# The second feed-forward layer's up products by seven products instead of eight

## The chip, the cores and the metric

The kernel runs on one core of a Trainium2 chip. The metric is the device time of one execution in microseconds; lower is better. A core has five engines with a queue of instructions each: PE multiplies matrices, DVE (VectorE), ACT (ScalarE) and POOL (GpSimd) work on elements, SP starts DMA transfers. An engine takes its queue in order; engines wait for each other by semaphores. SBUF is the working memory of 128 partitions; PSUM, with eight banks here, takes what PE writes.

## The reference

Two layers, each a mixer (pooling in the first, sparse attention in the second) and a gated feed-forward network (FFN) with a causal convolution of width 3. The tokens are 512 of a prompt (`hp`) and 8 x 8 new ones of running sequences (`hs`), 576 in all. The change concerns the FFN of the second layer.

```python
ALPHA = (2.0 * DEPTH) ** 0.25            # DEPTH = 2, D_MODEL = 1024, D_FF = 2816, CONV_W = 3
...
def conv_ffn(x, prefix, w_up, conv_w, conv_b, w_down):
    T = x.shape[1]
    up = x @ w_up                        # 1024 -> 2 * 2816: gate columns, then value columns
    up_pad = jnp.concatenate([prefix, up], 1)
    c = conv_b
    for k in range(CONV_W):
        c = c + conv_w[k] * up_pad[:, k:k + T]
    g, u = jnp.split(c, 2, -1)
    y = (jax.nn.silu(g) * u) @ w_down
    return y, up_pad[:, -(CONV_W - 1):]
...
        hp = layer_norm(ALPHA * hp + mp, ln_g[i, 0], ln_b[i, 0])
        hs = layer_norm(ALPHA * hs + ms, ln_g[i, 0], ln_b[i, 0])
        fp, nfp = conv_ffn(hp, zeros, ffn_w_up[i], ffn_conv_w[i], ffn_conv_b[i], ffn_w_down[i])
        fs, nfs = conv_ffn(hs, state_ffn[i], ffn_w_up[i], ffn_conv_w[i], ffn_conv_b[i], ffn_w_down[i])
        hp = layer_norm(ALPHA * hp + fp, ln_g[i, 1], ln_b[i, 1])
        hs = layer_norm(ALPHA * hs + fs, ln_g[i, 1], ln_b[i, 1])
```

## The kernel before

All products are in single precision made of parts: a matrix is split into a high part (a copy in the reduced type fp32r, by ACT) and a low part (the matrix less its high part, by DVE), and one product is three matmuls: high by high, high by low, low by high. The method `Units.split` with `pieces` (lines 247 and 248) splits weights, `mm3` (line 168) issues the matmuls. A matmul has a 128 x 128 block of weights standing and 288 tokens moving, which is half of the 576.

`x` lies transposed, features on partitions: `xz` is the residual (8 blocks of 128 features by 576 tokens), `xh` and `xl` its parts. In the first layer and in the second the function `ffn` does the same. The 2816 hidden features are 22 chunks of 128. `up` takes chunks by twos: it loads 256 gate columns and 256 value columns of the up weights (1024 KB each, one DMA each, into one of two raw buffers), splits them in pieces of 128 x 2048, and makes for each chunk, half of the tokens and side (gate or value) one bank of PSUM out of 8 blocks x 3 = 24 matmuls, so 96 matmuls for a chunk. `conv` copies the banks by ACT into the padded row buffer `u` (lines 405 to 407; four buffers), saves the last rows (POOL, line 408), and does the convolution: one ACT instruction (line 412) and two of DVE (413, 414) for each side. Then come SiLU (437, ACT), the product of the sides (438, DVE), and the split of the result into `hh` and `hl` (447 ACT, 448 DVE; eight buffers each).

`down` multiplies groups of four chunks (the last: six) with the down weights: for 8 blocks of output features and 2 halves of tokens 12 matmuls (the last: 18), and adds each bank to `xz` by DVE (line 494). The order is up of chunks 0 to 3, then up of the next four and down of the four before them, and so on; at the end up of 20 and 21 and the down of 16 to 21. During the first two chunks the layer norm of the second half of the tokens is still finished (`opening`), and during the last down the final norm of the first half is done (`closing`, from `final_norm`): it scales and shifts the rows `xn` with POOL on 352 of the columns and DVE on 672 at the same time (line 1606).

The program is written as a sequence of tiles and instructions; a planner then sets each engine's order from its own costs and the order of writing, and puts in the waits. `Slots` gives tiles of a tag in turn from a fixed number of buffers; a tile's next use waits until the last reader of the one before is done. PSUM tiles come from one pool of eight banks (`mmt`).

## Time and profile before

| | us |
|---|---|
| median of three runs | 1707.0 (1706.89 to 1708.22) |
| profiled execution, own time | 1708.67 |
| its span, first to last instruction | 1706.9 |
| PE busy | 1638.8 (96%) |
| DVE busy | 1046.9 (61%) |
| ACT busy | 816.3 (48%) |
| POOL busy | 426.5 (25%) |

The profile is one execution with start and length of each instruction. Busy time counts what the engine's units do; waiting for a semaphore is idle time, but what holds up an instruction after its start lengthens it. Matmuls overlap each other, so their spacing, not their length, says what one costs. The second FFN takes the stretch from about 1254 to 1686 us.

### The profile page before, as it was taken

To read this page: it belongs to the slowest core of one execution; us is meant where nothing else is said; L and a number is where in the kernel's file an instruction comes from. 1 tells how busy PE (TensorE), PEld (TensorE's weight loads), DVE (VectorE), ACT (ScalarE), POOL (GpSimd) and SP (SyncE) were. 2 spreads that over 40 slices of the span, in tenths; PEclk is the share of its full clock that TensorE was granted. 3 is DMA by queue.
4 is the path that set the end of the run, shared out by engine and by line. 5 is a ranking of instruction groups with operands and counts; after the bars stand their busy time and mean duration, and the time that the engine had idled before them with its cause. 6 is when DMAs were issued, how large, how long until landed. Compare 5 with 4: busy or idle time off the path is not lost. (4 is left out here: it accounts for less than half of the span.)

```text
span 1706.9 us, 31668 instructions
## 1 busy us (share of the span) xinstructions
PE 1638.8 (96%) x12711; PEld 1555.0 (91%) x12711; DVE 1046.9 (61%) x2162; ACT 816.3 (48%) x1499; POOL 426.5 (25%) x606
## 2 busy tenths in 40 slices
PE   7999999999999989999999988999999999999995
PEld 7999999999999989999956667887999999999995
DVE  7766464545574347889755558898466545454547
ACT  5654334343353314655654447888256534344331
POOL 2222121111020013333312216766023202111104
PEclk9999999999999999999999999999999999999998
DMA  5233132223247736544659941002512222222211
GB/s 190 83 100 100 55 111 83 75 75 99 63 167 214 229 119 244 187 167 164 208 182 350 342 124 26 1 12 69 153 50 75 78 96 75 84 90 81 93 60 56
DMA packets 130850, 206.02 MB, mean 121 GB/s; under 512 B 25775, under 2 KB 106761, under 8 KB 120336
## 3 DMA queue, kind: packets, MB, share of 16 engines
q1 hardware_dynamic: 120800, 134.49, 25.0%
q0 software_dynamic: 9216, 67.11, 11.1%
q8 instruction: 100, 1.64, 0.4%
q10 hardware_dynamic: 688, 2.40, 0.4%
q14 instruction: 46, 0.38, 0.1%
HBM read 179.63 MB, written 24.84 MB: 120 GB/s over the span
## 5 line engine op out<-in xcount | busy, mean ns | idle before, releaser
L168 PE MATMUL u<-xl,wha 128*128 128x288 f32 x704 | 208.0, 296 | 0.3 <-POOL xl L342 0.2
L168 PE MATMUL u<-xl,whb 128*128 128x288 f32 x704 | 208.0, 296 | 0.2
L168 PE MATMUL u<-xh,whb 128*128 128x288 f32 x704 | 207.3, 295 | 0.0
L168 PE MATMUL u<-xh,wha 128*128 128x288 f32 x704 | 207.3, 295 | 0.0
L168 PE MATMUL u<-xh,wlb 128*128 128x288 f32 x704 | 207.3, 295 | 0.0
L168 PE MATMUL u<-xh,wla 128*128 128x288 f32 x704 | 207.2, 295 | 0.0
L408 POOL COPY fcol<-u 128x18 f32<-128x18 f32 x88 | 69.4, 798 | 467.1 <-ACT u L407 467.0
L413 DVE SCALAR_TENSOR_TENSOR c<-u,convp,c 128x592 f32<-128x592 f32 x88 | 72.2, 831 | 122.2 <-ACT c L412 122.2
L248 DVE TENSOR_TENSOR wla<-rawa,wha 128x2048 fp32r<-128x2048 f32 (+1 forms) x52 | 99.5, 1918 | 68.7 <-ACT wha L247 68.0
L248 DVE TENSOR_TENSOR wlb<-rawb,whb 128x2048 fp32r<-128x2048 f32 x37 | 84.8, 2292 | 83.4 <-ACT whb L247 83.4
L168 PEld LDWEIGHTS u<-xl,wha 128*128 128x128 f32 x704 | 132.0, 188 | 2.0 <-DVE xl L342 1.1
L168 PEld LDWEIGHTS u<-xl,whb 128*128 128x128 f32 x704 | 132.0, 188 | 1.9 <-DVE xl L342 1.1
L168 PEld LDWEIGHTS u<-xh,whb 128*128 128x128 f32 x704 | 132.0, 188 | 0.1
L168 PEld LDWEIGHTS u<-xh,wha 128*128 128x128 f32 x704 | 132.0, 188 | 0.1
L168 PEld LDWEIGHTS u<-xh,wlb 128*128 128x128 f32 x704 | 132.0, 188 | 0.0
L168 PEld LDWEIGHTS u<-xh,wla 128*128 128x128 f32 x704 | 132.0, 188 | 0.0
L247 ACT ACTIVATE wha<-rawa 128x2048 fp32r<-128x2048 f32 (+1 forms) x52 | 83.0, 1615 | 91.1 <-PE d L168 58.9
L247 ACT ACTIVATE whb<-rawb 128x2048 fp32r<-128x2048 f32 x37 | 70.9, 1915 | 113.5 <-DMA rawb<-in_ffn_w_up 41.0
L494 DVE SCALAR_TENSOR_TENSOR xz<-xz,d 128x288 f32<-128x288 f32 x160 | 70.1, 450 | 85.5 <-PE d L168 84.8
L901 PE MATMUL pr<-xhi,W1h 128*128 128x256 f32 x512 | 105.6, 288 | 10.2 <-ACT xhi L874 10.2
L874 ACT ACTIVATE xhi<-xf 128x1024 fp32r<-128x1024 f32 (+1 forms) x68 | 70.1, 1031 | 83.1 <-PE pr L901 46.0
L168 PE MATMUL d<-hh,wha 128*128 128x288 f32 x352 | 104.4, 298 | 0.1
(779 smaller groups left out, 4900.6 us busy)
## 6 DMA issues: line engine op xcount, KB each, us to landing
rawa<-in_ffn_w_up SPq DMA_DIRECT2D x22, 1024.0 KB
rawb<-in_ffn_w_up SPq DMA_DIRECT2D x22, 1024.0 KB
rawa<-in_ffn_w_down SPq DMA_DIRECT2D x11, 1024.0 KB
rawb<-in_ffn_w_down SPq DMA_DIRECT2D x11, 1024.0 KB
rawa<-in_nsa_w_in SPq DMA_DIRECT2D x9, 1024.0 KB
sr<-in_state_win_kv SPq DMA_DIRECT2D x8, 1024.0 KB
out_win_kv_s<-sr SPq DMA_DIRECT2D x8, 1008.0 KB
rawb<-in_nsa_w_o SPq DMA_DIRECT2D x16, 256.0 KB
```

Source lines behind the costliest of these rows:

```text
L168: pe.matmul(out, a, b, start=first and j == 0, stop=last and j == n - 1)
L247: act.activation(h[:, a:b], r[:, a:b], AF.Copy)
L248: dve.tensor_tensor(lo[:, a:b], r[:, a:b], f32(h[:, a:b]), OP.subtract)
L408: pool.tensor_copy(col[:, :, m].rearrange("p (j i) -> p j i", i=2), u[:, TP:TP + 90].rearrange("p (j i) -> p j i", i=10)[:, :, 0:2])
L413: dve.scalar_tensor_tensor(c, u[:, 1:1 + CW], cv[:, 44 + m:45 + m], c, OP.mult, OP.add)
L494: dve.scalar_tensor_tensor(z, z, ALPHA if first else 1.0, p_[:, :HALF], OP.mult, OP.add)
L874: act.activation(xhi.rearrange(flat), xf.rearrange(flat), AF.Copy)
L901: pe.matmul(banks[b, kv][ri][:, :, gh * nn:(gh + 1) * nn], W1[wi][:, kv, ri * 8 + th * 4 + c], xx[:, c // 2, c % 2].rearrange("p g n -> p ...
```

## The change

The second layer's FFN becomes `ffn_seven`; the first keeps `ffn`. For chunks 2 to 21 the product of a 2 x 2 block matrix of weights (gate and value rows by two halves of the 1024 input features) with a 2 x 2 block matrix of tokens (two halves of the features by two halves of the tokens) is made with seven block products in place of eight, by sums and differences of blocks (the scheme of Strassen in Winograd's form). Each block product is 4 blocks x 3 = 12 matmuls of the same form as before. Chunks 0 and 1 (`up_plain`) are made with eight, and after them `token_sums` makes three combinations of the token blocks, once, in the raw buffers `u`.

For each chunk the weights come as four pieces of 128 x 512 (256 KB, one DMA each), POOL makes four combinations of them, and seven pieces are split by ACT and DVE. The pieces go through `Ring`: eight buffers for raw pieces and combinations, twelve pairs for the parts. Of the seven banks ACT copies three to SBUF; DVE makes three sums with a bank and one with a copy, and POOL and DVE put the four quarters of the result into `u`. The down weights come through the same ring in pieces of 128 x 512 (256 KB; the last down of 128 x 384, loaded anew for each half of the tokens). `hh` and `hl` get six buffers in place of eight. The order is up of 0 and 1, token sums, up of 2 to 5, then four times a down of four and an up of four, and the last down of six.

To make room, the constants behind `band` move to a tile that lives from the middle of the projection of the second layer on, with their DMA there, and the rows of the norms (`xn`) and the final norm's factors `gb` come from pools that are opened and closed around the chunks 2 to 21.

```diff
+HB = 6
+YB = 1
...
-    cst = cp.tile([128, CONSTS.shape[1] - (COFF["band"][1] - COFF["band"][0])], F32, name="cst")
     K0, K1 = COFF["band"]
+    cst = cp.tile([128, K0], F32, name="cst")
...
+    class Ring:
+        ORDER = "r" * 8 + "hl" * 12
+        def __init__(self, ctx, key):
+            self.slots, self.turn, self.n, self.key = {x: [] for x in "rhl"}, {x: 0 for x in "rhl"}, 0, key
+            for j, tag in enumerate(self.ORDER):
+                self.slots[tag].append(mkpool(ctx, f"ring{key}{tag}{j}"))
+        def slot(self, tag):
+            own = self.slots[tag]
+            j = self.turn[tag]
+            self.turn[tag] = (j + 1) % len(own)
+            self.n += 1
+            return own[j].tile([128, 512], F32 if tag == "r" else F32R, tag=tag, name=f"w{tag}{self.key}{self.n}")
+        def fetch(self, src):
+            _, k, n = src.shape
+            raw = self.slot("r")[:, :k * n]
+            sp.dma_start(raw.rearrange("p (k n) -> p k n", k=k), src)
+            return raw
+        def combine(self, a, b, op, out=None):
+            out = self.slot("r") if out is None else out
+            pool.tensor_tensor(out, a, b, op)
+            return out
+        def split(self, raw):
+            n = raw.shape[1]
+            h, lo = (self.slot(x)[:, :n] for x in "hl")
+            act.activation(h, raw, AF.Copy)
+            dve.tensor_tensor(lo, raw, f32(h), OP.subtract)
+            return tuple(t.rearrange("p (k n) -> p k n", n=128) for t in (h, lo))
...
+    def ffn_seven(l, R, ctx, opening, closing, no_norm, last_norm):
+        fp = Slots(ctx, f"ffn{l}")
+        cv = convp[l]
+        xz, xh, xl = X["z"], X["h"], X["l"]
...
+        half = [slice(0, HALF), slice(HALF, T)]
+        ks = [slice(0, 4), slice(4, 8)]
+        wv = I["ffn_w_up"][l].rearrange("(k p) n -> p k n", p=128)
+        def quarter(k, n):
+            return xh[:, ks[k], half[n]], xl[:, ks[k], half[n]]
+        def block(bank, w, x, first=True, last=True):
+            terms = [(w[wi][:, k], x[xi][:, k]) for k in range(4) for wi, xi in ((0, 0), (0, 1), (1, 0))]
+            mm3(bank[:, :HALF], terms, first, last)
+        def pieces(m):
+            return [R.fetch(wv[:, ks[k], c:c + 128]) for c in (m * 128, FF + m * 128) for k in range(2)]
...
+        def rows(m, q):
+            u = fp.tile([128, UW + 8], F32, tag="u", name=f"u{l}{q * NF + m}", bufs=4)
+            us = u[:, 2 + TP:UW].rearrange("p (b t) -> p b t", t=2 + TS)
+            pool.memset(u[:, 0:2], 0.0)
+            pool.tensor_copy(us[:, :, 0:2], sTv[:, :, q * NF + m].rearrange("p (b k) -> p b k", k=2))
+            return u, us[:, :, 2:]
...
+            hh = fp.tile([128, T], F32R, tag="hh", name=f"hh{l}{m}", bufs=HB)
+            hl = fp.tile([128, T], F32R, tag="hl", name=f"hl{l}{m}", bufs=HB)
...
+        def up_plain(ms):
+            w = {m: [R.split(p_) for p_ in pieces(m)] for m in ms}
+            banks = {}
+            for i, (n, m, q) in enumerate((n, m, q) for n in range(2) for m in ms for q in range(2)):
+                b = banks[m, n, q] = mmt(f"u{l}{m}{n}{q}")
+                for k in range(2):
+                    block(b, w[m][2 * q + k], quarter(k, n), k == 0, k == 1)
+                opening(i)
+            for m in ms:
+                us = []
+                for q in range(2):
+                    u, s = rows(m, q)
+                    act.activation(u[:, 2:2 + HALF], banks[m, 0, q][:, :HALF], AF.Copy)
+                    act.activation(u[:, 2 + HALF:2 + TP], banks[m, 1, q][:, :TP - HALF], AF.Copy)
+                    act.activation(s, samples(banks[m, 1, q]), AF.Copy)
+                    us.append(u)
+                gated(m, *us)
...
+        def token_sums(ctx):
+            tp_ = mkpool(ctx, f"tsum{l}", side="right")
+            z = [[xz[:, ks[k], half[n]] for n in range(2)] for k in range(2)]
+            t = {n: tuple(tp_.tile([128, 4, HALF], F32R, name=f"t{n}{x}{l}") for x in "hl") for n in (1, 2, 3)}
+            t[4] = quarter(0, 1)
+            for k in range(4):
+                raws = [fp.tile([128, UW + 8], F32, tag="u", name=f"ts{l}{k}{i}", bufs=4) for i in range(2)]
+                r = {n: raws[n % 2][:, i * HALF:(i + 1) * HALF] for i, ns in enumerate(((3, 2), (1, 4))) for n in ns}
+                for n, a, b in ((3, z[1][1][:, k], z[0][1][:, k]), (1, z[0][1][:, k], z[0][0][:, k]),
+                                (2, z[1][1][:, k], r[1]), (4, z[1][0][:, k], r[2])):
+                    (pool if n == 3 else dve).tensor_tensor(r[n], a, b, OP.subtract)
+                for n in (3, 2, 1, 4):
+                    act.activation(t[n][0][:, k], r[n], AF.Copy)
+                    dve.tensor_tensor(t[n][1][:, k], r[n], f32(t[n][0])[:, k], OP.subtract)
+            xt.update(t)
+        def up(m):
+            a11, a12, a21, a22 = pieces(m)
+            s1 = R.combine(a21, a22, OP.add)
+            s3 = R.combine(a11, a21, OP.subtract, a21)
+            s2 = R.combine(s1, a11, OP.subtract)
+            s4 = R.combine(a12, s2, OP.subtract)
+            w = {n: R.split(x) for n, x in (("a11", a11), ("s3", s3), ("s2", s2), ("a12", a12), ("a22", a22), ("s1", s1), ("s4", s4))}
+            (ug, sg), (uu, su) = rows(m, 0), rows(m, 1)
+            def product(n, wn, x):
+                bank = mmt(f"u{l}{m}p{n}")
+                block(bank, w[wn], x)
+                return bank
+            def copied(n, wn, x):
+                bank = product(n, wn, x)
+                out = fp.tile([128, HALF], F32, tag=f"y{n}", name=f"y{n}{l}{m}", bufs=YB)
+                act.activation(out, bank[:, :HALF], AF.Copy)
+                return out
+            def second(eng, u, us, a, b):
+                eng.tensor_tensor(u[:, 2 + HALF:2 + TP], a[:, :TP - HALF], b[:, :TP - HALF], OP.add)
+                eng.tensor_tensor(us, samples(a), samples(b), OP.add)
+            p1 = copied(1, "a11", quarter(0, 0))
+            p7 = copied(7, "s3", xt[3])
+            b6 = product(6, "s2", xt[2])
+            y = fp.tile([128, HALF], F32, tag="y", name=f"y{l}{m}", bufs=YB)
+            dve.tensor_tensor(y, p1, b6[:, :HALF], OP.add)
+            b2 = product(2, "a12", quarter(1, 0))
+            dve.tensor_tensor(ug[:, 2:2 + HALF], p1, b2[:, :HALF], OP.add)
+            pool.tensor_tensor(p7, y, p7, OP.add)
+            b4 = product(4, "a22", xt[4])
+            dve.tensor_tensor(uu[:, 2:2 + HALF], p7, b4[:, :HALF], OP.add)
+            p5 = copied(5, "s1", xt[1])
+            second(pool, uu, su, p7, p5)
+            pool.tensor_tensor(p5, y, p5, OP.add)
+            b3 = product(3, "s4", quarter(1, 1))
+            second(dve, ug, sg, p5, b3)
+            gated(m, ug, uu)
...
+        def down(chunks, first, last):
+            subs = [chunks] if len(chunks) == 4 else [chunks[:3], chunks[3:]]
+            wts = {}
+            for hf, m in ([(hf, m) for hf in range(2) for m in range(KD)] if last else [(hf, m) for m in range(KD) for hf in range(2)]):
+                if last or hf == 0:
+                    wts[m] = [R.split(R.fetch(I["ffn_w_down"][l][sub[0] * 128:(sub[-1] + 1) * 128, m * 128:(m + 1) * 128]
+                                              .rearrange("(k p) n -> p k n", p=128))) for sub in subs]
+                p_ = mmt(f"d{l}{m}{hf}{chunks[0]}")
+                mm3(p_[:, :HALF], [(wt[wi][:, k], hp[c][xi][:, half[hf]]) for sub, wt in zip(subs, wts[m])
+                                   for k, c in enumerate(sub) for wi, xi in ((0, 0), (0, 1), (1, 0))])
+                z = xz[:, m, half[hf]]
+                dve.scalar_tensor_tensor(z, z, ALPHA if first else 1.0, p_[:, :HALF], OP.mult, OP.add)
...
+        up_plain([0, 1])
+        no_norm()
+        with ExitStack() as c1:
+            token_sums(c1)
+            ups([2, 3])
+            ups([4, 5])
+            for g in range(4):
+                down(list(range(4 * g, 4 * g + 4)), g == 0, False)
+                ups(list(range(4 * g + 6, 4 * g + 10)))
+        last_norm()
         down(list(range(16, 22)), False, True)
...
+        N["cst"] = p_.tile([128, CONSTS.shape[1] - K1], F32, name="cstr")
+        sp.dma_start(N["cst"], I["consts"][:, K1:])
...
-    def final_norm(sp_, U):
-        gb = U.raw()[:, :2048].rearrange("p (s c) -> p s c", s=2)[:LT]
-        sp.dma_start(gb[:, 0], I["ln_g"][1, 1].unsqueeze(0).broadcast_to([LT, D]))
-        sp.dma_start(gb[:, 1], I["ln_b"][1, 1].unsqueeze(0).broadcast_to([LT, D]))
+    def final_norm(sp_):
+        gb = None
+        def open_last(ctx):
+            nonlocal gb
+            X["xn"] = mkpool(ctx, "xn2", side="right")
+            gb = X["xn"].tile([LT, 2, D], F32, name="gb")
+            sp.dma_start(gb[:, 0], I["ln_g"][1, 1].unsqueeze(0).broadcast_to([LT, D]))
+            sp.dma_start(gb[:, 1], I["ln_b"][1, 1].unsqueeze(0).broadcast_to([LT, D]))
...
-    U = Units(c0, "b")
+    cx = c0.enter_context(ExitStack())
+    X["xn"] = mkpool(cx, "xn1", side="right")
     norm = [Norm(lnp, 1, 0, hf) for hf in range(2)]
     steps = during_second_half(norm[0], 2)
     with ExitStack() as c1:
-        out_proj(U, c1, lambda hf, m: steps(m) if hf else None)
+        out_proj(Units(c1, "b"), c1, lambda hf, m: steps(m) if hf else None)
     norm[1].run(tile_steps(0))
+    closing, open_last = final_norm(lnp)
+    R = Ring(c0, 1)
     with ExitStack() as c1:
-        ffn(1, U, c1, during_first_half(norm[1]), final_norm(lnp, U))
+        ffn_seven(1, R, c1, during_first_half(norm[1]), closing, cx.close, lambda: open_last(c0))
```

## Rows read from the trace of the kernel before

**Rows 1.** The page's parts 1 and 3: engines; then one DMA queue.

```profile
PE 1638.8 (96%) x12711; PEld 1555.0 (91%) x12711; DVE 1046.9 (61%) x2162; ACT 816.3 (48%) x1499; POOL 426.5 (25%) x606
...
q1 hardware_dynamic: 120800, 134.49, 25.0%
```

**Rows 2.** Stretches: length, busy PE, PEld, DVE, ACT, POOL; clock, DMA share, GB/s.

```profile
1060.00:1180.00 120.00, 112.64 (x736) 98.92 (x736) 107.99 (x359) 107.10 (x303) 84.41 (x111) 1.00 0.05 11
...
1287.00:1642.00 355.00, 355.00 (x2680) 355.00 (x2679) 184.89 (x235) 149.50 (x248) 55.60 (x117) 1.00 0.26 84
1642.00:1687.00 45.00, 44.79 (x345) 44.25 (x344) 31.10 (x61) 10.80 (x17) 11.12 (x11) 1.00 0.20 60
```

**Rows 3.** The chain that ended last, 1250 to 1707: start, us, what.

```profile
1362.61 25.49 PE d L168 x192
1388.09 50.88 PE u L168 x384
```

**Rows 4.** Groups on DVE, 1250 to 1707: busy us, mean ns, idle before.

```profile
L248 DVE TENSOR_TENSOR wlb<-rawb,whb 128x2048 fp32r<-128x2048 f32 x31 | 71.1, 2292 | 79.2 <-ACT whb L247 79.2
L414 DVE SCALAR_TENSOR_TENSOR c<-u,convp,c 128x592 f32<-128x592 f32 x44 | 35.7, 832 | 0.8
L413 DVE SCALAR_TENSOR_TENSOR c<-u,convp,c 128x592 f32<-128x592 f32 x44 | 35.7, 831 | 56.3 <-ACT c L412 56.3
L494 DVE SCALAR_TENSOR_TENSOR xz<-xz,d 128x288 f32<-128x288 f32 x80 | 34.6, 450 | 37.7 <-PE d L168 37.5
L438 DVE TENSOR_TENSOR c<-c,c 128x592 f32<-128x592 f32 x22 | 17.0, 773 | 1.1
...
L448 DVE TENSOR_TENSOR hl<-c,hh 128x512 fp32r<-128x512 f32 x22 | 15.2, 692 | 11.9 <-ACT hh L447 11.9
...
L448 DVE TENSOR_TENSOR hl<-c,hh 128x64 fp32r<-128x64 f32 x22 | 4.8, 219 | 0.0
```

**Rows 5.** DVE in order of time, 1274 to 1345: start, us, what.

```profile
1290.10 1.57 DVE L414 SCALAR_TENSOR_TENSOR c<-u,convp,c 128x592 f32<-128x592 f32 x2
...
1310.38 2.29 DVE L248 TENSOR_TENSOR wlb<-rawb,whb 128x2048 fp32r<-128x2048 f32 x1 [4.57 <-ACT whb L247]
1312.59 1.57 DVE L413 SCALAR_TENSOR_TENSOR c<-u,convp,c 128x592 f32<-128x592 f32 x2
```

**Rows 6.** Groups on POOL, whole span: busy us, mean ns, idle before.

```profile
L408 POOL COPY fcol<-u 128x18 f32<-128x18 f32 x88 | 69.4, 798 | 467.1 <-ACT u L407 467.0
...
L342 POOL TENSOR_TENSOR xl<-xz,xh 128x288 fp32r<-128x288 f32 x18 | 15.4, 857 | 51.0 <-DVE xh L340 46.7 <-issue 4.2
...
L1532 POOL TENSOR_TENSOR xl<-osum,xh 128x512 fp32r<-128x512 f32 x8 | 10.2, 1280 | 3.3 <-ACT xh L1531 3.3
```

**Rows 7.** POOL in order of time, 1254 to 1345: start, us, what.

```profile
1310.76 2.73 POOL L408 COPY fcol<-u 128x18 f32<-128x18 f32 x2 [6.42 <-ACT u L407]
```

**Rows 8.** Line 1606, the whole span: ns min/median/max, first and last start.

```profile
L1606 POOL TENSOR_TENSOR xn<-xn,rawb x12: 922/1418/1536, 1670.1 to 1699.4; 96x352 f32<-96x352 f32 x12
L1606 DVE TENSOR_TENSOR xn<-xn,rawb x12: 845/1463/1603, 1670.7 to 1700.1; 96x672 f32<-96x672 f32 x12
```

**Rows 9.** POOL and DVE in order of time at the end: start, us, what.

```profile
1692.39 8.41 POOL L1606 TENSOR_TENSOR xn<-xn,rawb 96x352 f32<-96x352 f32 x6 [2.01 <-ACT xn L328]
...
1693.01 8.51 DVE L1606 TENSOR_TENSOR xn<-xn,rawb 96x672 f32<-96x672 f32 x6 [1.67 <-ACT xn L328]
```

**Rows 10.** Groups on ACT, 1250 to 1707: busy us, mean ns, idle before.

```profile
L405 ACT ACTIVATE u<-u 128x288 f32<-128x288 f32 x44 | 17.8, 408 | 38.0 <-PE u L168 38.0
...
L447 ACT ACTIVATE hh<-c 128x512 fp32r<-128x512 f32 x22 | 13.9, 632 | 21.1 <-DVE c L438 21.1
```

**Rows 11.** ACT in order of time, 1274 to 1300: start, us, what.

```profile
1281.71 0.70 ACT L437 ACTIVATE c<-c 128x592 f32<-128x592 f32 x1
1282.32 0.87 ACT L412 ACTIVATE c<-u,convp 128x592 f32<-128x592 f32 x1
```

**Rows 12.** SP's queue in order of time, 1388 to 1440: start, us, what.

```profile
1392.27 0.37 SPq L225 DMA_DIRECT2D rawb<-in_ffn_w_up  x1
```

More of the change, by code (lines that the diff above doesn't have):

```diff
@@ L505, in ffn, with samples, conv, gated @@
         down(list(range(16, 22)), False, True)
+    def ffn_seven(l, R, ctx, opening, closing, no_norm, last_norm):
+        fp = Slots(ctx, f"ffn{l}")
+        cv = convp[l]
+        xz, xh, xl = X["z"], X["h"], X["l"]
+        sT = fp.tile([128, 704], F32, name=f"fsT{l}")
+        c0_ = ExitStack()
+        state = mkpool(c0_, f"fst{l}").tile([128, 6, 128], F32, name=f"fst{l}")
+        srows = I["state_ffn"][l].rearrange("b k (m p) -> (b k m) p", p=128)
+        sp.dma_start(state[:, 0:5], srows[0:640].rearrange("(j p) c -> p j c", p=128))
+        sp.dma_start(state[0:64, 5], srows[640:704])
+        for q in range(2):
+            pt = tpt(f"fsp{l}{q}")
+            n = 0
+            for j in range(q * 4, min(q * 4 + 4, 6)):
+                rows = 128 if j < 5 else 64
+                transpose(pt[:, n:n + rows], state[:rows, j])
+                n += rows
+            act.activation(sT[:, q * 512:q * 512 + n], pt[:, :n], AF.Copy)
+        c0_.close()
+        sTv = sT.rearrange("p (r m) -> p r m", m=44)
+        col = fp.tile([128, 18, 44], F32, name=f"fcol{l}")
+        hp, xt = {}, {}
+        half = [slice(0, HALF), slice(HALF, T)]
[14 more added lines that the diff above has]
+            return u, us[:, :, 2:]
+        def samples(t):
+            return t[:, TP - HALF:HALF].rearrange("p (b t) -> p b t", t=TS)
+        def conv(m, u):
+            pool.tensor_copy(col[:, :, m].rearrange("p (j i) -> p j i", i=2),
+                             u[:, TP:TP + 90].rearrange("p (j i) -> p j i", i=10)[:, :, 0:2])
+            cf = fp.tile([128, UW], F32, tag="c", name=f"c{l}{m}", bufs=4)
+            c = cf[:, 0:CW]
+            act.activation(c, u[:, 2:UW], AF.Identity, bias=cv[:, 132 + m:133 + m], scale=cv[:, 88 + m:89 + m])
+            dve.scalar_tensor_tensor(c, u[:, 1:1 + CW], cv[:, 44 + m:45 + m], c, OP.mult, OP.add)
+            dve.scalar_tensor_tensor(c, u[:, 0:CW], cv[:, m:m + 1], c, OP.mult, OP.add)
+            return cf
+        def gated(m, ug, uu):
+            cg, cu = conv(m, ug), conv(NF + m, uu)
+            act.activation(cg[:, 0:CW], cg[:, 0:CW], AF.Silu)
+            dve.tensor_tensor(cu[:, 0:CW], cg[:, 0:CW], cu[:, 0:CW], OP.mult)
+            hh = fp.tile([128, T], F32R, tag="hh", name=f"hh{l}{m}", bufs=HB)
+            hl = fp.tile([128, T], F32R, tag="hl", name=f"hl{l}{m}", bufs=HB)
+            def views(full):
+                return (full[:, 0:TP], full[:, TP:].rearrange("p (b t) -> p b t", t=TS))
+            cs = (cu[:, 0:TP], cu[:, 2 + TP:2 + TP + 80].rearrange("p (b t) -> p b t", t=10)[:, :, 0:TS])
+            for hv, lv, s in zip(views(hh), views(hl), cs):
+                act.activation(hv, s, AF.Copy)
+                dve.tensor_tensor(lv, s, f32(hv), OP.subtract)
+            hp[m] = (hh, hl)
+        def up_plain(ms):
[8 more added lines that the diff above has]
+                us = []
+                for q in range(2):
+                    u, s = rows(m, q)
[55 more added lines that the diff above has]
+            gated(m, ug, uu)
+        def ups(ms):
+            for m in ms:
+                up(m)
+        colf = col.rearrange("p r m -> p (r m)")
+        op_, os_ = (O[n][l].rearrange(pat, p=128) for n, pat in
+                    (("ffn_p", "b k (m p) -> (b k m) p"), ("ffn_s", "b k (m p) -> (b k m) p")))
+        def state_out(q):
+            pt = tpt(f"fco{l}{q}")
+            n = min(4, 7 - q * 4)
+            ob = fp.tile([128, UW + 8], F32, tag="u", name=f"fob{l}{q}", bufs=4)[:, 0:512]
+            for j in range(n):
+                w = min(128, 792 - (q * 4 + j) * 128)
+                transpose(pt[:w, j * 128:(j + 1) * 128], colf[:, (q * 4 + j) * 128:(q * 4 + j) * 128 + w])
+            if q == 0:
+                act.activation(ob, pt, AF.Copy)
+                sp.dma_start(op_, ob[0:88, 0:128])
+                sp.dma_start(os_[0:40], ob[88:128, 0:128])
+                sp.dma_start(os_[40:424].rearrange("(j p) c -> p j c", p=128), ob[:, 128:512].rearrange("p (j c) -> p j c", c=128))
+            else:
+                act.activation(ob[:, 0:256], pt[:, 0:256], AF.Copy)
+                act.activation(ob[0:24, 256:384], pt[0:24, 256:384], AF.Copy)
+                sp.dma_start(os_[424:680].rearrange("(j p) c -> p j c", p=128), ob[:, 0:256].rearrange("p (j c) -> p j c", c=128))
+                sp.dma_start(os_[680:704], ob[0:24, 256:384])
+        def down(chunks, first, last):
[10 more added lines that the diff above has]
+                dve.scalar_tensor_tensor(z, z, ALPHA if first else 1.0, p_[:, :HALF], OP.mult, OP.add)
+                if last:
+                    closing(hf, m)
+                    if hf == 0 and m in (3, 5):
+                        state_out(m // 4)
+        up_plain([0, 1])
[8 more added lines that the diff above has]
+        last_norm()
+        down(list(range(16, 22)), False, True)
```

12 lines of the change are left out of this document (6 added, 6 removed).

## The prediction

> **What bounds the kernel now.** I read the page's first part, then the stretches, the chain that ended last, and the groups of each engine. The page shows PE busy for 96% of the span [rows 1]. A busy PE is not yet a bound, so the stretches come next: from 1287 to 1642 us PE is busy all of the 355 us, at a granted clock of 1.00 (2.4 GHz), with DVE at 185, ACT at 150 and POOL at 56 us [rows 2]. The chain agrees: one up of four chunks is 384 matmuls in 50.88 us without a break, one down 192 in 25.49 us [rows 3]. So a matmul of this form costs 50.88 / 384 = 132.5 ns, and in the second FFN every matmul less is that much less, as long as the others keep up. They have room: DVE works 52% of this stretch. That room is what the change spends.
>
> **What it removes.** 20 chunks lose 96 - 84 = 12 matmuls each: 240 x 132.5 ns = **31.8 us**. Blocks and moving columns keep their form, so I keep the spacing. Chunks 2 to 21 with four downs are 20 x 96 + 4 x 192 = 2688 matmuls, 356.2 us; they become 2448, **324.4 us**.
>
> **What it adds on DVE.** Durations are from [rows 4]; where instructions follow each other the next starts about 0.09 us before the last ends (two of 0.83 take 1.57 [rows 5]), so I take 0.09 off each. A chunk: seven splits of 128x512 at 0.60 (4.21 us), four convolution steps at 0.74 (2.97), the product of the sides 0.68, the low part of the result 0.60 + 0.13, three sums of 288 with a bank at 0.36 (1.08), and the last quarter 0.29 + 0.13 (224 and 64 elements, between the rows of 64 and 288). Sum 10.1 us. A down: 16 x 0.36 + 8 x 0.60 = 10.6 us. Over the stretch 20 x 10.1 + 4 x 10.6 = **244 us** of 324: alone it would hide.
>
> **What it adds on POOL, and what that does to DVE.** Before, POOL does small copies here. Now each chunk has four combinations of 512 at 1.28, two sums of 288 at 0.86, and one quarter of 224 and 64 at about 0.74 and 0.43 (line through the two rows): 8.0 us, and about 3 us of copies [rows 6]. POOL itself has 324 / 20 = 16 us per chunk. But the two engines hold each other up. Two POOL copies of 18 elements began at 1310.76, inside a 2.29 us DVE split, and took 2.73 us, until the second DVE instruction had begun [rows 5, 7]. At the end both work on pieces of `xn`: alone the POOL piece takes 922 and the DVE piece 845 ns [rows 8], together six pairs take 8.41 and 8.51 us, 1.42 a pair [rows 9]. Alone DVE would need 6 x 0.755 + 0.09 = 4.62 us; so each POOL piece of 352 cost DVE 0.65 us, 1.84 ns an element. A chunk has 4 x 512 + 2 x 288 + 224 + 64 = 2912 such elements: **0 to 5.36 us** of waiting on DVE per chunk. The lower end is POOL working while DVE is idle or adds from a bank; for those sums I see no row with a hold-up. Of DVE's 12.75 us per chunk (a quarter of a down counted in) 2.94 are sums with a bank; so 77% of POOL's holds meet DVE in an instruction that can be held, and some meet it idle: I take 3.7 us. DVE then needs 244 + 20 x 3.7 = **318 us** (bounds 244 and 351).
>
> The Trainium skill, page "SBUF — State Buffer", section "Who interferes with whom", states this as an exclusive lock: a DVE instruction with two SBUF inputs and a GpSimd one that reads SBUF can't run at once, and the second to come is blocked until the first is over. The pairs agree that the two exclude each other; they differ in the size, since 0.65 us of a 922 ns piece is charged and not all of it. With the whole instruction the price would be 8.0 us per chunk: the fourth rival.
>
> **What two equally loaded engines lose.** PE at 324 and DVE at 318 us can't both be full all the time. The nearest row is the attention stage, 1060 to 1180 us: DVE 108.0, ACT 107.1 and POOL 84.4 of 120 us, and PE busy 112.6, 94% [rows 2]. The other end is the FFN now, 100%. Here the twelve pairs of parts let weights be split eleven products (17 us) ahead, and eight banks hold PE's results, which is deeper than a chain of softmax steps; still DVE is fuller. I take 95%: 324.4 / 0.95 = 341.5, **17.1 us lost** (0 to 21).
>
> **The start.** Token sums use the four `u` buffers, which chunks 0 and 1 hold until their convolutions are done; chunk 1's last ended at 1291.7 [rows 5], and PE has done chunk 1 by about 1287, its first new product by 1288.6. Two of the four feature blocks then follow, each a chain of DVE, ACT and DVE of about 3 us (0.45 three times, 0.41, 0.45 and the passing on [rows 4, 10]): until 1297.7. PE could wait 9 us. The planner can move up the products that need no token sum (two more of chunk 2, two of chunk 3; 1.59 us each): 2.7 us of waiting are left. It does reorder: SiLU of the gate ran at 1281.71, ahead of the value's convolution, which is written before it [rows 11]. I take **5 us** (2.7 to 9).
>
> **The end.** The last down loads and splits 32 pieces of 384 where there were three of 2048: on DVE about 32 x 0.47 = 15 for 3 x 2.2 = 6.6 us. From 1642 to 1687 DVE worked 31 of 45 us [rows 2], most in the second half where the first norm runs, so 8 more fit only if split ahead; six steps fit in the ring. **2 us** (0 to 5).
>
> **What costs nothing.** ACT gets three more copies of 512 per chunk (0.63) and gives up some of 0.41 [rows 10]: 150 us become about 185 of 340, and its idle time covers that. DMA: a group of four chunks and a down is 6 MB in 12,288 packets of 512 bytes; priced as the mean packet of now (25.0% of 16 engines for 1706.9 us over 120,800 packets, 56 ns of 1.1 KB [rows 1]) that is 43 us of the 70 us that PE works on the group. SP issues 24 transfers in it at 0.37 us [rows 12], 9 us, behind nothing but ring buffers that come free in order. Without this cover PE would wait for the rest of the 256 KB in hand, 512 packets, under 2 us. The moved constants (0.75 MB at the queue's 315 GB/s while busy, 2.4 us) stand in SP's queue in the projection: 0, at most 2.4.
>
> **Sum.** 1708.7 (the profiled execution: span 1706.9 and 1.8 around it) - 31.8 + 17.1 + 5 + 2 = 1701.0. The median of the runs lies 1.7 lower: **1699**, its own range 1690 to 1706.
>
> **Rivals.**
> 1. *PE stays the bound.* POOL's holds fall where DVE is idle. For it: DVE alone needs 244 of 324. Against: it needs nearly every hold to miss. -31.8 + 7 gives 1682.
> 2. *Start and end eat the gain.* PE isn't given other products and waits 9 us at the token sums, 5 at the end: -31.8 + 17.1 + 14 gives 1706, no change. For it: five steps in a row there pass from engine to engine. Against: the planner's order above.
> 3. *Slower: DVE becomes the bound, in the up of each four chunks, through POOL's holds.* If each hold meets a DVE that wants to go on, DVE needs 351 us and, with 5% idle for its own waits (for POOL's sums above all, behind which the next additions queue), 370, against 356 before: +14 + 7 gives 1728. It decides from 4.4 us of hold per chunk on: (0.95 x 349 - 244) / 20. For it: combinations run back to back, as the pieces at the end do. Against: a quarter of DVE's work reads a bank.
> 4. *The whole POOL instruction blocks.* 244 + 20 x 8.0 = 404 us on DVE: +48 + 7 gives 1762. Against it stand the 0.65 us above.
>
> That the matmuls don't go away is no rival; they are written out.
>
> **How the numbers follow.** Forecast 0.42, rivals 0.15, 0.13, 0.25 and 0.05. A measurement tells 0.2%, 3.4 us, from no change: the forecast lies below 1703.6 for 0.36 of its 0.42, and with rival 1 and a little of 2 that makes faster 0.53; same 0.16, from the forecast's upper end and rival 2; slower 0.31. The range 1680 to 1730 takes in rivals 1 to 3 and leaves out some 0.15.
>
> **What would show it.** PE has 240 matmuls fewer, spaced 132 ns where it doesn't wait. In the stretch of chunks 2 to 21 DVE is busy over 90%, its splits of 512 last 0.69 at the shortest and over 1.2 us where POOL holds; the sums with a bank stay at 0.45. If these splits all stay near 0.7, holds are rare and rival 1 should be the time; if PE waits above 30 us there, rival 3. A wait of PE near 1290 gives the start. It would be wrong if PE is held by something with no price here, say weights that land late.

## The result, and the profile after

The changed kernel takes **1731.0 us** (median of 4 runs, 1727.7 to 1733.0), the kernel before 1707.6 beside it: 1.0128 times as long, interval 1.0099 to 1.0156. The forecast was 1699. The profiled execution took 1732.98 us, its span is 1731.2. The first line of the page already says what happened (busy us, share of the span, instructions):

```profile
PE 1629.9 (94%) x12471; PEld 1539.8 (89%) x12471; DVE 1208.1 (70%) x2469; ACT 860.4 (50%) x1634; POOL 616.6 (36%) x770
```

The 240 matmuls are gone (12711 in [rows 1]), and yet PE's busy time fell by 9 us only, and the span grew. So PE has longer matmuls and more gaps. The stretches of the second FFN show where. Columns as in [rows 2]; from the third line on a down and an up of four chunks alternate, the last line but one is the last down, and the last one sums up chunks 2 to 21 with four downs:

```profile
1291.00:1320.00 29.00, 24.71 (x150) 22.62 (x148) 25.53 (x51) 17.82 (x42) 14.20 (x23) 0.88 0.09 27
1320.00:1357.00 37.00, 30.04 (x192) 27.71 (x190) 30.68 (x45) 19.42 (x36) 22.73 (x31) 0.91 0.29 85
1357.00:1383.00 26.00, 25.09 (x189) 25.09 (x190) 22.83 (x39) 9.49 (x17) 10.83 (x14) 1.00 0.31 89
1383.00:1430.00 47.00, 45.17 (x336) 44.50 (x336) 38.72 (x60) 23.51 (x45) 32.82 (x37) 1.00 0.34 98
1430.00:1462.00 32.00, 27.71 (x195) 27.24 (x194) 31.96 (x47) 14.14 (x26) 19.96 (x23) 0.95 0.25 72
1462.00:1507.00 45.00, 45.00 (x341) 45.00 (x340) 40.92 (x59) 24.80 (x47) 31.30 (x35) 1.00 0.35 102
1507.00:1538.00 31.00, 27.44 (x193) 26.94 (x193) 26.97 (x45) 11.84 (x21) 19.56 (x22) 0.94 0.21 61
1538.00:1583.00 45.00, 45.00 (x340) 45.00 (x340) 41.87 (x58) 25.43 (x48) 32.73 (x35) 1.00 0.34 100
1583.00:1613.00 30.00, 27.06 (x190) 26.57 (x189) 26.19 (x43) 11.22 (x21) 18.80 (x22) 0.94 0.22 62
1613.00:1658.00 45.00, 45.00 (x340) 45.00 (x340) 40.79 (x59) 25.18 (x49) 29.52 (x34) 1.00 0.30 88
1658.00:1709.00 51.00, 45.95 (x335) 45.19 (x333) 40.98 (x89) 21.43 (x41) 13.71 (x15) 0.93 0.40 114
1291.00:1658.00 367.00, 342.23 (x2449) 335.67 (x2448) 326.46 (x500) 182.84 (x349) 232.44 (x272) 0.97 0.28 82
```

The reader is to see three things. The ups from 1462 on are full: 336 matmuls in 45 us at clock 1.00, as short as the smaller count allows. The loss sits in the first two lines (chunks 2 to 5), in three of the four downs (192 matmuls in 31 to 32 us against 25.49 in [rows 3]), and in the last down. And in those lines the granted clock is under 1.00: part of them ran at 1.2 GHz, while [rows 2] have 1.00 from 1287 to 1687. With PE's segments, before and after, measured from the start of the first matmul of a kind to the end of the last, and "loss" as what a segment took beyond its matmuls at 132.5 ns:

| us | before | after | change |
|---|---|---|---|
| 240 matmuls fewer | | | -31.8 |
| first up begins | 1254.6 | 1257.9 | +3.2 |
| loss in chunks 0 to 5 (before: 0 to 7) | 6.2 | 28.8 | +22.6 |
| loss in the other ups | 0.7 | 3.9 | +3.2 |
| four downs | 102.6 | 120.9 | +18.3 |
| last down | 43.4 | 50.6 | +7.2 |
| from there to the end | 21.0 | 22.6 | +1.5 |
| sum (spans: +24.3) | | | +24.2 |

On DVE, the groups from 1291 to 1709 (busy us, mean ns, idle before) answer to [rows 4]:

```profile
L287 DVE TENSOR_TENSOR wl<-wr,wh 128x512 fp32r<-128x512 f32 x164 | 145.1, 908 | 10.2 <-ACT wh L286 9.8
L600 DVE SCALAR_TENSOR_TENSOR c<-u,convp,c 128x592 f32<-128x592 f32 x43 | 43.3, 1040 | 0.0
...
L731 DVE SCALAR_TENSOR_TENSOR xz<-xz,d 128x288 f32<-128x288 f32 x78 | 32.6, 443 | 5.0 <-PE d L170 5.0
L606 DVE TENSOR_TENSOR c<-c,c 128x592 f32<-128x592 f32 x22 | 21.7, 987 | 4.0 <-ACT c L605 3.8
L616 DVE TENSOR_TENSOR hl<-c,hh 128x512 fp32r<-128x512 f32 x22 | 21.0, 954 | 0.2 <-ACT hh L615 0.2
```

Most of the forms whose two inputs lie in SBUF became much longer (832 to 1040, 773 to 987, 692 to 954 ns, the splits 692 to 908), L599 hardly (831 to 848); the sum with a PSUM bank stayed at 443. With the rows of 64 (646 ns against 219) and of L599, each excess times its count, that is 65 us, 3.2 per chunk. Such a lengthening is called a hold here. The combinations pay too, 1599 ns where the row alone had 1280 [rows 6]; the same stretch on POOL:

```profile
L280 POOL TENSOR_TENSOR wr<-wr,wr 128x512 f32<-128x512 f32 x72 | 114.8, 1599 | 68.1 <-DMA wr<-in_ffn_w_up 46.2 <-DVE wl L287 9.8 <-DVE y L681 4.9
```

How a hold becomes a lost down is best read at the second one, 1507 to 1538. POOL in order of time (start, us, what):

```profile
1506.54 5.36 POOL L280 TENSOR_TENSOR wr<-wr,wr 128x512 f32<-128x512 f32 x2 [2.17 <-DVE c L600]
...
1512.67 2.65 POOL L280 TENSOR_TENSOR wr<-wr,wr 128x512 f32<-128x512 f32 x2
1515.28 0.79 POOL L684 TENSOR_TENSOR y<-y,y 128x288 f32<-128x288 f32 x1
```

DVE at the same time:

```profile
1509.73 2.25 DVE L616 TENSOR_TENSOR hl<-c,hh 128x512 fp32r<-128x512 f32 x2
1511.90 0.73 DVE L287 TENSOR_TENSOR wl<-wr,wh 128x512 fp32r<-128x512 f32 x1
1516.10 0.45 DVE L686 TENSOR_TENSOR u<-y,u113p 128x288 f32<-128x288 f32 x1 [3.46 <-POOL y L684]
1516.47 2.83 DVE L287 TENSOR_TENSOR wl<-wr,wh 128x512 fp32r<-128x512 f32 x3
```

And PE:

```profile
1514.80 0.29 PE L170 MATMUL d<-hh,wl 128*128 128x288 f32 x1
1516.61 0.40 PE L170 MATMUL d<-hh,wh 128*128 128x288 f32 x1 [1.52 <-DVE u L686]
...
1523.74 0.40 PE L170 MATMUL d<-hh,wh 128*128 128x288 f32 x1 [2.04 <-DVE xz L731]
```

The sum `p7 = y + p7` (L684) of the chunk in hand stands in POOL's queue behind four combinations for a coming chunk, two of them stretched to 5.36 us together beside DVE's two-input work (the later two took 2.65). DVE's next instruction needs that sum and waits 3.46 us. PE waits for that instruction (1.52 us); behind it in DVE's queue are splits, which read two SBUF inputs, and the additions that free the banks of the down, for which PE waits another 2.04 us. The first of the three lost downs, 1430 to 1462, has no such wait of DVE: there DVE is at work for 31.96 of 32 us, and PE waits for it all the same. What the engines waited for from 1383 to 1658 (total us, times, longest), first PE:

```profile
PE d L170 <- DVE xz L731: 5.7, 3, 2.0
PE d L170 <- DVE y L681: 2.7, 1, 2.7
PE d L170 <- DVE u L686: 2.4, 2, 1.5
```

and DVE:

```profile
DVE u L686 <- POOL y L684: 12.2, 6, 3.5
DVE wl L287 <- ACT wh L286: 9.6, 7, 3.3
DVE u L674 <- POOL y L689: 4.3, 4, 1.7
```

Before, PE has no such wait at all from 1362 to 1642.

### The profile page after: what moved, and what is told of

Its sections match the earlier page's. It is cut to its first block, busy times and chain, and to the rows that moved or that the text cites. A ratio compares the mean times of both kernels' runs of the same rounds, so it can differ in the third digit from the quotient of the medians.

```text
span 1731.2 us, 32397 instructions
## 1 busy us (share of the span) xinstructions
PE 1629.9 (94%) x12471; PEld 1539.8 (89%) x12471; DVE 1208.1 (70%) x2469; ACT 860.4 (50%) x1634; POOL 616.6 (36%) x770
## 5 line engine op out<-in xcount | busy, mean ns | idle before, releaser
L287 DVE TENSOR_TENSOR wl<-wr,wh 128x512 fp32r<-128x512 f32 (+1 forms) x212 | 176.7, 856 | 14.0 <-ACT wh L286 13.4
L286 ACT ACTIVATE wh<-wr 128x512 fp32r<-128x512 f32 (+1 forms) x212 | 123.6, 607 | 110.6 <-POOL wr L280 45.3
L280 POOL TENSOR_TENSOR wr<-wr,wr 128x512 f32<-128x512 f32 x80 | 127.1, 1594 | 71.1 <-DMA wr<-in_ffn_w_up 46.2
L170 PE MATMUL d<-hh,wh 128*128 128x288 f32 x352 | 107.9, 308 | 15.2 <-DVE xz L731 5.7
L170 PE MATMUL d<-hh,wl 128*128 128x288 f32 x352 | 107.1, 304 | 1.1 <-DVE wl L287 1.1
L170 PE MATMUL d<-hl,wh 128*128 128x288 f32 x352 | 107.0, 304 | 0.5 <-DVE hl L616 0.5
L1731 POOL TENSOR_TENSOR P<-P,st 128x512 f32<-128x512 f32 (+1 forms) x125 | 89.0, 743 | 44.9 <-DVE st L1725 25.5
L1116 DVE STREAM_TRANSPOSE xf<-cr 128x512 f32<-128x512 f32 x128 | 84.7, 691 | 28.7 <-POOL xlo L1120 23.6
L1145 PE MATMUL pr<-xlo,W1h 128*128 128x256 f32 x512 | 104.1, 285 | 0.0
L170 PE MATMUL d<-hl,wha 128*128 128x288 f32 x352 | 103.9, 295 | 0.0
```

Of the source, the lines that this page charges most:

```text
L170: pe.matmul(out, a, b, start=first and j == 0, stop=last and j == n - 1)
L280: pool.tensor_tensor(out, a, b, op)
L286: act.activation(h, raw, AF.Copy)
L287: dve.tensor_tensor(lo, raw, f32(h), OP.subtract)
L1116: dve.transpose(xf[:, :, :, :, 32 * q:32 * q + 32].rearrange("p t d g n -> p t g d n"), src)
L1145: pe.matmul(banks[b, kv][ri][:, :, gh * nn:(gh + 1) * nn], W1[wi][:, kv, ri * 8 + th * 4 + c], xx[:, c // 2, c % 2].rearrange("p g n -> p ...
```

## Experiments

Each ratio is to the kernel before, run beside it on the same chip (its medians there: 1707.6 to 1709.9 us). "Early loss" is that of chunks 0 to 5, and the downs are the four before the last; these and the splits are of the one profiled execution.

| kernel | us | ratio [95%] | early loss | four downs | last down | mean split, ns |
|---|---|---|---|---|---|---|
| before | 1707.6 | 1 | 6.2 | 102.6 | 43.4 | |
| changed | 1731.0 | 1.0128 [1.0099, 1.0156] | 28.8 | 120.9 | 50.6 | 903 |
| e_plainring | 1709.7 | 0.9996 [0.9978, 1.0013] | 6.2 | 102.6 | 43.3 | 687 |
| e_nocombine | 1692.3 | 0.9889 [0.9854, 0.9923] | 16.3 | 103.6 | 44.9 | 749 |
| e_memset | 1699.3 | 0.9939 [0.9922, 0.9956] | 20.4 | 103.6 | 46.4 | 748 |
| e_dvecombine | 1707.6 | 0.9988 [0.9969, 1.0006] | 25.9 | 103.4 | 50.7 | 736 |
| e_dveall | 1699.3 | 0.9945 [0.9926, 0.9965] | 23.7 | 103.5 | 44.0 | 682 |
| h_sumsdve | 1721.8 | 1.0064 [1.004, 1.0089] | 31.4 | 109.2 | 50.3 | 852 |
| e_notoken | 1679.7 | 0.983 [0.9805, 0.9855] | 6.3 | 103.1 | 44.0 | 687 |
| e_warm4 | 1721.0 | 1.0053 [1.003, 1.0076] | 16.7 | 121.9 | 50.6 | 880 |
| f_dve_warm4 | 1701.6 | 0.996 [0.9944, 0.9975] | 15.6 | 106.4 | 50.7 | 733 |
| f_dve_warm4_tail | 1696.6 | 0.9941 [0.9923, 0.9959] | 14.4 | 105.4 | 43.3 | 733 |
| g_dveall_warm4 | 1693.7 | 0.9904 [0.9885, 0.9924] | 15.1 | 107.0 | 43.4 | 686 |

**e_plainring**: is it the pieces, the ring, the second read of weights?

```diff
-            for m in ms:
-                up(m)
+            for m0 in ms[::2]:
+                up_plain([m0, m0 + 1])
...
-            token_sums(c1)
```

> All 22 chunks by eight products, without combinations and token sums, but with the ring, the small pieces, the down weights loaded anew, and the moved tiles of the changed kernel. Rival C (ring, pieces, reload): 1725 or more. Theories A and B: PE is the bound again, 1707 plus the 4 us that the FFN begins later and the 7 us that the last down is longer: 1707 to 1718.

0.9996. Pieces, ring, reload and moved constants cost nothing. Only the 1.5 us after the last down appear here too.

**e_nocombine**: no work of POOL on weights.

```diff
-            s1 = R.combine(a21, a22, OP.add)
-            s3 = R.combine(a11, a21, OP.subtract, a21)
-            s2 = R.combine(s1, a11, OP.subtract)
-            s4 = R.combine(a12, s2, OP.subtract)
+            s1, s3, s2, s4 = a21, a21, a11, a12
```

> Leaves out POOL's four combinations per chunk: the products use the raw pieces in their place, so the output is another one; DVE, ACT and PE have the same instructions as the changed kernel. Theory A (POOL's holds on DVE are the price): the splits of 512 fall from 0.86 us on the mean to about 0.70, the downs go back from 31 to 25.5 us, and the time falls from 1731 to about 1705. Rival B (DVE's own added work and its order, no holds): under 5 us are won, about 1727. Rival C (small pieces, ring and reloaded down weights): the same, about 1727.

0.9889: without combinations the scheme gains 1.1%, 18 to 19 us, more than expected; the downs are full again. The early loss falls to 16.3 us and doesn't go away.

**e_memset**: POOL keeps its place in the chain, but hardly reads.

```diff
-            pool.tensor_tensor(out, a, b, op)
+            pool.tensor_tensor(out[:, 0:8], a[:, 0:8], b[:, 0:8], op)
+            pool.memset(out[:, 8:512], 0.0)
+            pool.memset(out[:, 8:512], 0.0)
+            pool.memset(out[:, 8:136], 0.0)
```

> Each combination on POOL becomes a combination of 8 of the 512 columns and three fills of the rest with zeros (496, 496 and 128 elements), so the output is another one. POOL is as long at work in the chain from piece to split (about 1.2 to 1.4 us in place of 1.28), and DVE waits for the same POOL results, but POOL reads almost nothing of SBUF meanwhile. Theory A (POOL's reading holds DVE's two-input instructions): near the kernel without combinations, 1692 to 1700, splits of 512 near 0.75. Rival D (DVE, in its order, waits for POOL's results, which come late in the chain of piece, four combinations, split): as the changed kernel, 1722 to 1731.

0.9939. POOL from 1288 to 1676:

```profile
L281 POOL MEMSET wr<- 128x504 f32 x72 | 37.3, 518 | 49.2 <-DVE wl L290 29.4 <-DMA wr<-in_ffn_w_up 19.6
...
L280 POOL TENSOR_TENSOR wr<-wr,wr 128x8 f32<-128x8 f32 x72 | 33.4, 465 | 5.1 <-DVE wl L290 2.4 <-ACT hh L618 1.8 <-DMA wr<-in_ffn_w_up 0.6
```

and DVE's splits beside it:

```profile
L290 DVE TENSOR_TENSOR wl<-wr,wh 128x512 fp32r<-128x512 f32 x164 | 120.3, 754 | 14.4 <-ACT wh L289 12.6
```

As long on POOL (1.70 us a combination with its three fills, against 1.60), but hardly any reading: the splits fall from 908 to 754 ns and the downs are full. And DVE waits for POOL's sums no less than in the changed kernel. Its waits over the ups and downs from 1374.1 to 1630.3, and PE's only one:

```profile
DVE u L689 <- POOL y L687: 13.1, 6, 3.5
DVE u L677 <- POOL y L692: 10.8, 8, 2.7
PE d L170 <- DVE xz L734: 0.7, 1, 0.7
```

So neither the length of the chain through POOL nor DVE's waits for it cost PE its time by themselves; the holds have to be there too. The Trainium skill, page "SBUF — State Buffer", section "Who interferes with whom", says the same of both sides: a DVE instruction with two SBUF inputs contends with a GpSimd one that reads SBUF, not with one that only writes. By the same section of that page of the Trainium skill a DVE instruction with at most one SBUF input, outside its 2-port modes, doesn't contend (the 443 ns of L731).

**e_dvecombine**, **e_dveall** and **h_sumsdve** make, with the changed kernel, a table of two by two: combinations on POOL or DVE, sums of products on POOL or DVE.

```diff
-            pool.tensor_tensor(out, a, b, op)      # e_dvecombine, e_dveall
+            dve.tensor_tensor(out, a, b, op)
...
-            pool.tensor_tensor(p7, y, p7, OP.add)  # e_dveall, h_sumsdve
+            dve.tensor_tensor(p7, y, p7, OP.add)
...
-            second(pool, uu, su, p7, p5)
-            pool.tensor_tensor(p5, y, p5, OP.add)
+            second(dve, uu, su, p7, p5)
+            dve.tensor_tensor(p5, y, p5, OP.add)
```

> The four combinations of a chunk run on DVE instead of POOL, the result is the same. DVE gets 20 x 4 x 0.60 = 48 us more work of its own and is rid of holds of up to 80 x 0.94 = 75 us. Theory A: splits of 512 back near 0.70, DVE full but never held long, 1715 to 1725. Rival B (DVE's own work is the bound): 1750 to 1775, since 48 us come on top. Rival C: 1731, no change.

> As the kernel with the combinations on DVE (1707.6), and also the two sums of 288 and the quarter of 224 and 64 of each chunk on DVE; POOL has only its small copies. DVE gets 20 x (2 x 0.36 + 0.42) = 23 us more of its own and is rid of holds of at most 20 x 864 x 1.84 ns = 32 us. Theory A: 1700 to 1710, nearly balanced. Rival B (DVE's own work): 1720 to 1730.

> The four combinations of a chunk stay on POOL, the sums on POOL (p7, p5 and the last quarter of the value) go to DVE, so no product's sum stands behind combinations in POOL's queue any more. DVE's own work grows by 0.36 + 0.36 + 0.29 + 0.13 = 1.1 us a chunk, and POOL's holds fall by 864 elements x 1.84 ns = 1.6 us a chunk, so by load alone nothing changes. Theory Q (the downs lose because the value's sum waits on POOL behind combinations of the next chunks, and DVE and then PE behind it): the downs of 30.7 to 32.0 us go back to 25.6 to 27.5, and a part of the 21 us lost in chunks 2 to 5 with them: 1704 to 1714. Theory H (the downs lose because combinations hold DVE's own instructions, wherever the sums are): downs stay above 30 us, splits of 512 stay near 0.9 us, 1725 to 1733.

| | sums on POOL | sums on DVE |
|---|---|---|
| combinations on POOL | 1.0128 | 1.0064 |
| combinations on DVE | 0.9988 | 0.9945 |

Each of the three is a gain. e_dvecombine came below both ranges given for it (theory A had the sign, not the size), e_dveall just below theory A's. Moving the combinations is worth 0.0140 and 0.0119, moving the sums 0.0064 and 0.0043. In h_sumsdve the downs fall to 109.2 us, two thirds of the way to 103.4, as theory Q had it. The total falls by as much, 11 us, and no further: early loss and last down stay, and splits, at 852 ns, are still held. Neither theory had its number. (Its profiled execution took 8 us more than its median; it came to the FFN 8 us late, which lies before the table's segments.) The plainest row of the study is e_dveall's from 1375.3 to 1630.5, three downs and four ups:

```profile
1375.30:1630.50 255.20, 255.20 (x1922) 255.20 (x1921) 244.51 (x488) 140.13 (x260) 45.75 (x86) 1.00 0.32 91
```

The same 1920 matmuls took the changed kernel 274.9 us, with DVE busy 247.5 (1383.2 to 1658.1). DVE works as long in both, and its work is a *larger share* here, 96% against 90%, and PE waits for nothing. DVE's groups here, 1288 to 1676:

```profile
L287 DVE TENSOR_TENSOR wl<-wr,wh 128x512 fp32r<-128x512 f32 x164 | 109.0, 683 | 1.4 <-ACT wh L286 0.9
L280 DVE TENSOR_TENSOR wr<-wr,wr 128x512 f32<-128x512 f32 x72 | 48.4, 684 | 6.9 <-DMA wr<-in_ffn_w_up 6.8
```

A combination costs DVE 684 ns when DVE does it itself. On POOL it took 1599 ns, and what it saved DVE came back as holds, 37 us in the splits alone (164 x (908 - 683)) against the 48.4 of all 72 combinations; DVE's 247.5 against 244.5 us say that, with the sums, nothing was saved.

What differs is what DVE waits for between its instructions. Over the same 1920 matmuls, 254.4 us of PE's work at 132.5 ns (us; the last column adds the four before it):

| kernel | length | DVE at work | waits for POOL | for ACT | for a load | sum |
|---|---|---|---|---|---|---|
| changed | 274.9 | 247.5 | 16.5 | 9.6 | | 273.6 |
| h_sumsdve | 261.8 | 251.5 | | 9.7 | | 261.2 |
| e_dvecombine | 256.1 | 236.3 | 11.5 | | 7.9 | 255.7 |
| e_dveall | 255.2 | 244.5 | | 2.7 | 6.3 | 253.5 |
| e_memset | 256.2 | 208.4 | 23.9 | 9.6 | | 241.9 |

Where the sum lies above PE's 254.4 us, the stretch is as long as the sum within 1.3 us: DVE, with its holds and its waits in order, is the bound. Where it lies below, PE is, and even more waiting costs next to nothing. Holds without waits for POOL's sums (h_sumsdve) cost 7 us, waits without the combinations' holds (e_memset) 2 at most, both together 20. This is an account of one execution of each kernel; the waits for ACT hold some that ACT itself owes to PE, which it doesn't part.

**e_notoken**: what of the early loss is the token sums' (the sums are left out, and products with them take unsummed tokens), on e_dveall:

```diff
-        token_sums(c1)
+        xt.update({1: quarter(0, 1), 2: quarter(1, 1), 3: quarter(1, 1), 4: quarter(0, 1)})
```

> As the kernel with all combinations and sums on DVE, but leaves out the token sums: the products use quarters of the tokens in their place, so the output is another one. It takes away 28 DVE instructions (about 11 us), their holds, and the wait for them. If the start (17 us over PE's own work) comes from the token sums: the first six chunks fall from 93.7 to about 80 us, 1685 to 1688. If it comes from the gating of chunks 0 and 1 and the first splits and combinations: 90 us, 1695 to 1697.

0.983, another 20 us off e_dveall; better than expected. The early stretch then is:

```profile
1288.00:1331.50 43.50, 43.50 (x329) 43.50 (x329) 43.47 (x89) 28.84 (x55) 16.52 (x22) 1.00 0.28 81
```

and with the token sums, in e_dveall, the same 330 matmuls:

```profile
1288.00:1349.00 61.00, 51.57 (x330) 48.71 (x329) 53.85 (x114) 35.11 (x71) 16.49 (x30) 0.89 0.20 59
```

So 17.5 us of e_dveall's early loss are the token sums; PE's clock of 0.89 is a part of it. Whether it is their work on DVE or their wait for the row buffers, this run doesn't tell: it takes away both.

**e_warm4**, **f_dve_warm4**, **f_dve_warm4_tail**: fewer chunks by seven products, where PE has to wait (the edit abridged; the norm's steps stay with chunks 0 and 1).

```diff
         up_plain([0, 1])
+        up_plain([2, 3])          # e_warm4; f_dve_warm4 with e_dvecombine's edit
...
-        ups([2, 3])
...
+        ups([18, 19]); up_plain([20, 21])   # f_dve_warm4_tail, the last group
```

> Chunks 0 to 3 by eight products in place of 0 and 1; token sums stand behind chunks 2 and 3. PE gets 24 matmuls more, 3.2 us. If the 21 us lost on chunks 2 to 5 are the wait for token sums behind the row buffers of chunks 0 and 1 (start), most of it stays, since the sums again wait for the buffers of the chunks just before them: 1731 to 1735. If they are the pile of work on DVE while the norm ends (the second half's back steps, two chunks of gating, token sums), the pile is spread: 1718 to 1725.

> Combinations on DVE and chunks 0 to 3 by eight products. With the combinations on DVE the first six chunks still take 95.9 us for some 78 of PE's work. If the two gains add (23 and 10 us off 1731, less what they share at the start): 1698 to 1702, faster than before. If they are the same gain: 1706 to 1711.

> The same with chunks 20 and 21 by eight products, too (PE 3.2 us more). With the combinations on DVE the last down takes 50.7 us, without any 44.9; PE waits there for the last chunk's hidden values. If that is DVE's pile of work from the last up, this wins 6 - 3 us: 1695 to 1699. If it is the down weights loaded anew for each half, it loses 3: 1702 to 1705.

Two chunks more by eight products take 12 us off the early loss (28.8 to 16.7) and cost 24 matmuls, 3.2 us: 1.0053, in the range given for a pile of work on DVE that is spread. With combinations on DVE they take 10 us off (25.9 to 15.6), and the first down after them is 3.9 us longer: 0.996 against 0.9988. The last chunks by eight bring the last down back to 43.3 us, as in e_plainring: the pieces of the down's weights aren't what made it late. In f_dve_warm4_tail one quarter of the tokens of chunks 20 and 21 already held a token sum, so these two chunks multiply other numbers; the work is the same.

**g_dveall_warm4**: e_dveall and e_warm4 together, the version to which the runs pointed.

> All combinations and sums on DVE, and chunks 0 to 3 by eight products. With POOL out of the way the first six chunks still take 93.7 us (PE has 70 of matmuls and 6 of the norm's transposes in them). In the kernel with POOL's combinations the two more chunks by eight products won 10 us at the start for 3 us of matmuls. If the pile at the start is DVE's own work, as theory A with rival B for this stretch has it: 4 to 8 us are won, 1691 to 1695. If the start is set by the row buffers that the token sums wait for: 3 us are lost, 1702.

**1693.7 us**, 0.9904 [0.9885, 0.9924]: faster than both kernels, by 1% of the kernel before, and in the range expected if the pile at the start is DVE's own work; for the row buffers 1702 was expected. The early loss falls from 23.7 to 15.1 us, and the first down after it is 4.4 us longer than a full one.

## Why the prediction was wrong

**What it removes** was right: 240 matmuls, and 44.9 us for an up of 336 wherever PE doesn't wait.

**DVE's own work and POOL's holds** were right within their bounds: 3.2 us of hold per chunk against 3.7, and DVE busy 326 us in chunks 2 to 21 with four downs, against 318 and some 10 us of token sums that were not in that sum. The signs named beforehand came: splits of 0.69 and of over 1.2 us, sums with a bank unchanged, a wait of PE near 1290. DVE's share, forecast over 90%, was 89% (326.5 of 367.3).

**Two steps failed, the start by size and the loss of two equally loaded engines by kind.** The profiled execution took 32 us more than the sum's 1701.0. If the 17.1 us are shared out by matmuls, 15 of the 32 lie in chunks 0 to 5 (22.6 came, 5 + 2.3 were there), 7 in the rest up to the last down (21.5 for 14.8), 5 in the last down (7.2 for 2), and 5 before the first up and after the last down, where there was no term (3.2 and 1.5).

**What two equally loaded engines lose.** It took 95% from the attention stage and put 17.1 us on the whole stretch, start apart at 5. Chunks 2 to 21 with four downs took 367.3 us for 324.4 of matmuls: 42.9 lost, where the two terms had 22.1. The term made the loss a matter of how large DVE's share of work is. e_dveall shows a larger share and PE losing nothing. In the table over 1920 matmuls the loss is that by which DVE's work, holds included, and its waits in order for POOL and ACT together exceed PE's time: 273.6 us against 254.4. The work alone, at 247.5, would have fitted; the waits for POOL alone cost next to nothing in e_memset, where the work was 208.4. What PE then waits for are the additions that free its banks, behind held splits of up to 1.8 us, and its clock falls with these waits. The prediction asked, for matmul and DMA, what is queued behind; for POOL's sums it gave this half a sentence, inside the third rival.

**The start** had 5 us (2.7 to 9). The wait that it priced came, 2.9 us for the sums' parts from 1291 to 1300; the rest came behind it. e_dveall against e_notoken shows 17.5 for the token sums alone. The chain of five steps was priced by its own durations; what was left out is that convolutions and splits stand between these steps in DVE's queue, that PE lacks later splits 25 us on (from 1318 to 1335), and the clock, 0.88 and 0.91:

```profile
PE u13p L170 <- DVE wl L287: 4.0, 3, 1.9
```

How much of this each of the three makes was not separated. Whether token sums in buffers of their own would save it wasn't tried.

**The end** had 2 us for splitting 32 pieces. Those cost nothing (e_plainring 43.3 us); what came was 7.2 us, most of it one wait of PE for the last chunk's `hh` (1658 to 1709, total, times, longest):

```profile
PE d L170 <- ACT hh L615: 4.4, 1, 4.4
```

The additions, the convolution and the parts of that chunk alternate on DVE, POOL and ACT. The loss goes with combinations and sums both on DVE (44.0), and nearly with combinations that don't read (44.9 and 46.4 in e_nocombine and e_memset), hardly with one of the two moved (50.3, 50.7); why one isn't enough stays open.

**Before the first up** there was no term. From the last matmul of the projection to the first up it takes 6.4 us in the changed kernel and 7.1 in h_sumsdve, and 2.6 to 3.3 in the kernel before and in every other run. Only in these two does POOL make whole combinations there, four in 6.13 us, and PE waits 3.6 us for a sum of DVE (L1824) that stands behind held work:

```profile
1247.76 6.13 POOL L280 TENSOR_TENSOR wr<-wr,wr 128x512 f32<-128x512 f32 x4 [1.34 <-DVE wl L287]
```

So these 4 us go with POOL's combinations, too. (Other runs also reach the first up late, as e_plainring and e_memset do; there the projection took longer, 61 and 64 us against 59.) The 1.5 us after the last down come in every run with the ring; their cause is open.

**The clock** had no term. The six stretches above with a clock under 1.00 sum to 31 us at 1.2 GHz ((1 - clock) x length / 0.5), of which PE loses at most half, 16 us.

**What costs nothing** was right for ACT (183 of 367 us) and SP, and PE waits for no load itself. But ahead of the downs at 1507 and 1583 the chain that ended last runs through a load of weights of 3.2 and 3.3 us, which began when a split gave its ring buffer free and for which POOL's combinations, and the sum behind them, waited. More ring buffers were not tried.

**The rivals.** Rival 3 had the time (1728) and most of the mechanism: DVE becomes the bound by POOL's holds and by its own waits for POOL's sums. Its parts were off: 3.2 us of hold a chunk, under its threshold of 4.4, and waits of 10% of the stretch in place of 5; and the loss shows in the downs, not in the ups of four chunks, which are full. The time is partly luck, since of the loss 22.6 us lie at the start, where it had 5. Rival 2 had two of the places, start and end, with 9 and 5 us for 22.6 and 7.2. Rival 4 (1762) fell: 3.2 us a chunk, not 8.0. Rival 1 failed as long as POOL combines; in e_notoken, without combinations on POOL and without token sums, its full PE is seen.
